# Two-block attention network on one core: input norm's broadcast in two operand parts, final root by Ln and Exp, attention values taken as full pairs of 128 columns

## The chip, the cores and the metric

The kernel runs on one core of a Trainium2 chip. A core has five engines that each work through their own instruction queue: TensorE (matrix products and transposes, its products go to the accumulation memory PSUM), VectorE, ScalarE, GpSimd and SyncE (SP), which here only issues transfers. Transfers between the chip's memory and the on-chip buffers are issued from the queues of SP, ScalarE and GpSimd. The engines wait for each other through semaphores. The metric is the time of one execution on the device, in microseconds (us), and the median over runs is compared. In the views PE is TensorE's products, PEld its loads of the stationary operand, DVE VectorE, ACT ScalarE, POOL GpSimd.

## The reference

The input x has 512 tokens of 1024 features. It is normalized (mean and variance, gain and shift of 1024 elements each) and goes through two layers of a first block and one layer of a second block.

```python
h = _layernorm(x, ln_in_g, ln_in_b)
for layer in range(2):
    proj = h @ w_in[layer]            # aq ak av ag, bq bk bv bf bg, cq ck cv cg
    # a: 4 heads of differential attention, values of 128
    # b: 4 heads of forgetting attention, heads of 64
    #    softmax(q k^T * scale + cum_q - cum_k, causal) @ v
    # c: 4 heads of stick-breaking attention, heads of 64
    #    weights = exp(log_sigmoid(z) + sum of log_sigmoid(-z) over later keys); weights @ v
    y = concat(ya, yb, yc) @ w_out[layer]      # each gated by silu
    h = _layernorm(DEEPNORM_ALPHA * h + y, ln_g[layer], ln_b[layer])
# second block: three mixers (dsa, hgrn2, mla), a gated sum, and a gated feed-forward part
#    mla: s = (q_nope . k_nope + q_pe . k_pe) * scale, q_nope of 128, q_pe of 64; k_pe is one for all 4 heads
x = x + mixed @ w_out_2
x = x + (silu(h @ w_gate) * (h @ w_up)) @ w_down
return rms_norm(x, final_norm)
```

All of it is in float32. `rms_norm` divides by the root of the mean of squares plus 1e-6.

## The kernel before, in words

Tokens are worked in four tiles of 128 (`NT` = 4), and the 1024 features in eight groups of 128 (`KD` = 8). A projection is made in three products of reduced-precision operands: each operand is split into a high part (a cast by ScalarE, line 203 for weights) and a low part (a subtraction by VectorE, line 204), and `mm3` (lines 217 to 219) adds high x high, high x low and low x high. Weights come through SP's queue (line 199) into three buffers `wraw`. Products of attention scores with values, and the transposes ahead of them, are made in full float32.

A scheduler plans a fixed order for each engine from the order of the program and priorities; `self.after(x, y)` only demands that x stands behind y in the order of issue. Generators interleave the side work (an attention mechanism) with main work (projections) at fixed rates (`merge`). `Steps` holds the attention back in stages: the scores of one step, then the transposes of the step before, then the products with the values of the step before that.

**Start.** `start` loads x by tiles through SP, and the gain and shift of the input norm through ScalarE's queue as 16 rows of 128 (line 403). Sixteen float32 products (line 411) broadcast these rows to all partitions, into four PSUM banks: `g` in two halves of 512 features, and `b` in two. `norm` makes each tile's statistics: for tile 0 by VectorE (line 427), for the others by sums on ScalarE (line 423) and squares (line 312). `root` takes an approximate inverse root by Ln and Exp on ScalarE (lines 270 and 272) and one correction on VectorE. Four VectorE passes follow (lines 319 and 320, each once for each half). The tile is then transposed (line 293), split (line 297) and projected to the values of mechanism b. `hgrn_bounds`, for the second block, loads two small vectors through ScalarE's queue (lines 441 and 452) and has some eight tiny instructions; the planner has set them at the beginning.

**b and c.** `att_b` takes its 4 heads in 2 pairs. A pair has one PSUM bank `pv` (the tag has one buffer): head 0 of the pair fills partitions 0 to 63, head 1 partitions 64 to 127, for 512 tokens. For each of the 4 token tiles, and in it for each head, the product with the values is made from 64 columns of v (line 787, made in line 1093). After both heads of a pair, `out_bc` multiplies the whole bank by the gate (line 563), and `finish` splits the result. `att_c` goes head by head, each in four key tiles, and puts its products with 64 columns of v into the pair's bank (lines 848 and 852); `out_bc` follows after the second head (line 565).

**mla.** The scores are two products: 128 rows of q and k (line 1372), and the rope part of 64 rows (line 1373). The rope key `kpe` stands twice in one tile, in partitions 0 to 63 and 64 to 127, since the heads' rope queries stand in pairs.

**End.** In `ffn` each of the 4 column groups of 256 adds up its products for the 4 token tiles. In the last third of each group VectorE adds the residual (line 1450), ScalarE squares and sums (line 920), and VectorE multiplies by the gain (line 1452). After the last group `rms_scale` reduces the four sums (line 909), scales them (line 911) and iterates the inverse root three times (`rsqrt`, lines 241 to 265); then ScalarE scales one half of the tile (line 1456) and VectorE the other (line 1458), and both go out.

Of the kernel before, what the change touches and what calls it, by code (L numbers as in the profile page):

```python
# [21 lines left out]
P = 128  # L22
# [13 lines left out]
class Net:  # L36
    def __init__(self, ctx, tc, a, out):
# [8 lines left out]
        self.bounds = None  # L46
# [220 lines left out]
    def root(self, y, s, n, eps, x):  # L267
# [5 lines left out]
        nc.vector.tensor_scalar(x, s, -0.5 / n, -0.5 * eps, op0=ALU.mult, op1=ALU.add)  # L273
        nc.vector.scalar_tensor_tensor(x, y, x, y, op0=ALU.mult, op1=ALU.mult)
        nc.vector.scalar_tensor_tensor(y, x, 1.5, y, op0=ALU.add, op1=ALU.mult)

# [29 lines left out]
    def layernorm(self, x, g, b, eps, mv, sums=True):  # L306

        nc = self.nc
        if sums:
            nc.vector.tensor_scalar(mv[:, 2:3], mv[:, 0:1], mv[:, 1:2], -1.0 / D, op0=ALU.add, op1=ALU.mult)  # L310
            sq = self.wa([P, D], BF16)
            nc.scalar.activation(sq, x, AF.Square, bias=mv[:, 2:3], accum_out=mv[:, 3:4])
            self.root(mv[:, 5:6], mv[:, 3:4], D, eps, mv[:, 4:5])
        else:
            nc.vector.tensor_scalar_mul(mv[:, 2:3], mv[:, 0:1], -1.0)
            self.root(mv[:, 5:6], mv[:, 1:2], 1, eps, mv[:, 4:5])
        for half in range(2):
            y = x[:, half * S:(half + 1) * S]
            nc.vector.scalar_tensor_tensor(y, y, mv[:, 2:3], g[half], op0=ALU.add, op1=ALU.mult)
            nc.vector.scalar_tensor_tensor(y, y, mv[:, 5:6], b[half], op0=ALU.mult, op1=ALU.add)  # L320
# [48 lines left out]
    def values(self, l, hT, w=None, pool=None):  # L369
# [6 lines left out]
        w = w or self.weights(self.src1(l, "bv", 0, 260), 260, pool=pool)  # L376
# [4 lines left out]
        def step(t):  # L381
# [3 lines left out]
            ps = self.proj_n(w, 260, hT, t)  # L385
# [6 lines left out]
    def start(self, hT):  # L392
# [3 lines left out]
        self.roots()  # L396
# [16 lines left out]

        def norm(t):
# [14 lines left out]
            self.layernorm(xs[t], g, b, 1e-5, st, sums=t > 0)  # L429
# [1405 lines left out]
```

## Time and profile before

| | |
|---|---|
| time, median of 3 runs | 1658.45 us (1657.46 to 1660.41) |
| the profiled execution's own time | 1661.47 us |
| its span in the profile | 1659.7 us |
| TensorE busy | 1618.0 us (97%), 9320 products |
| VectorE busy | 1045.5 us (63%), 2281 instructions |
| ScalarE busy | 734.5 us (44%), 1507 instructions |
| mean granted TensorE clock | 0.994 |

A product's record lasts longer than it holds the engine: records overlap, and their ends are modelled, so a busy engine is not an engine at its peak. The distance between starts tells what a record costs the next one. A float32 product stands as two records. Idle time of an engine that is not the bottleneck costs nothing.

### The profile page before, as it was taken

What the parts mean: (1) busy time and instruction counts of PE and PEld (TensorE: products, weight loads), DVE (VectorE), ACT (ScalarE), POOL (GpSimd) and SP (SyncE); (2) the same over time, 40 slices, a digit from 0 to 9 for tenths busy, and PEclk for the clock granted to TensorE, in tenths of its full rate; (3) what the DMA queues carried; (4) which work ended last, traced back from release to release, by engine and by line L of the source; (5) the groups of instructions that cost most, each with busy time, mean ns of one, the idle gap of its engine ahead of it and who ended that gap; (6) DMA issues with size and microseconds to landing.
All of it is one profiled execution on the core that took longest, in us unless ns stands there. A gap on an engine that the chain in (4) does not pass through costs nothing.

```text
span 1659.7 us, 24221 instructions
## 1 busy us (share of the span) xinstructions
PE 1618.0 (97%) x9320; PEld 1374.3 (83%) x9320; DVE 1045.5 (63%) x2281; ACT 734.5 (44%) x1507; POOL 67.0 (4%) x117
## 2 busy tenths in 40 slices
PE   6999999999999999899999999999999999999997
PEld 6878787987777979788889866788889988888997
DVE  7686878884567797836999996433446434434233
ACT  4455654443465644556545765422333322322222
POOL 1021000100000000000000001100000000000000
PEclk9999999999999999999999999999999999999999
DMA  7443132341121413432012321223443533333221
GB/s 230 143 164 107 33 111 75 103 154 56 51 77 39 128 61 122 138 89 79 24 39 69 90 64 52 83 83 108 147 126 105 162 102 101 102 102 96 96 92 61
DMA packets 141884, 160.33 MB, mean 97 GB/s; under 512 B 14101, under 2 KB 131109, under 8 KB 141257
## 3 DMA queue, kind: packets, MB, share of 16 engines
q1 hardware_dynamic: 135960, 141.34, 27.7%
q0 software_dynamic: 2944, 12.13, 2.1%
q10 hardware_dynamic: 2864, 5.32, 1.0%
q8 instruction: 73, 1.20, 0.3%
q14 instruction: 43, 0.34, 0.1%
HBM read 143.55 MB, written 15.21 MB: 96 GB/s over the span
## 4 chain that ended last, share of the span: by engine, by line
PE 83%; DVE 8%; ACT 2%; DMA 1%; issue 1%; ACTq 0%; DVEq 0%
PE pj L218 19%; PE pj L217 19%; PE pj L219 19%; PE pv L1093 3%; PE tr L732 2%; PE s L217 2%; PE s L218 2%; PE s L219 2%; PE s L718 2%; PE s L1685 2%; PE s L719 1%; PE s L837 1%; DVE wlo L204 1%; DMA wraw<-in_w_in_dram 1%; PE pv L848 1%
## 5 line engine op out<-in xcount | busy, mean ns | idle before, releaser
L218 PE MATMUL pj<-hTl,whi 128*128 128x512 f32 (+1 forms) x1136 | 440.8, 388 | 0.0
L217 PE MATMUL pj<-hTh,whi 128*128 128x512 f32 (+1 forms) x1136 | 440.2, 388 | 0.0
L219 PE MATMUL pj<-hTh,wlo 128*128 128x512 f32 (+1 forms) x1136 | 439.6, 387 | 0.2 <-DVE wlo L204 0.2
L204 DVE TENSOR_TENSOR wlo<-wraw,whi 128x1024 fp32r<-128x1024 f32 (+3 forms) x237 | 269.4, 1143 | 240.7 <-ACT whi L203 235.5
L203 ACT CAST whi<-wraw 128x1024 fp32r<-128x1024 f32 (+3 forms) x237 | 228.9, 979 | 333.3 <-PE pj L218 196.8
L217 PEld LDWEIGHTS pj<-hTh,whi 128*128 128x128 f32 x1136 | 213.6, 188 | 45.3 <-issue 6.6
L218 PEld LDWEIGHTS pj<-hTl,whi 128*128 128x128 f32 x1136 | 213.6, 188 | 43.4 <-issue 4.8
L219 PEld LDWEIGHTS pj<-hTh,wlo 128*128 128x128 f32 x1136 | 213.6, 188 | 42.9 <-issue 3.8
L217 PE MATMUL pj<-whi,hTh 128*128 128x256 f32 (+2 forms) x352 | 101.2, 288 | 3.4 <-ACT whi L208 2.7
L219 PE MATMUL pj<-whi,hTl 128*128 128x256 f32 (+2 forms) x352 | 101.9, 290 | 0.0
L218 PE MATMUL pj<-wlo,hTh 128*128 128x256 f32 (+2 forms) x352 | 101.1, 288 | 0.0
L219 PE MATMUL pj<-whi,t2k 128*128 128x256 f32 x304 | 85.7, 282 | 0.0
L218 PE MATMUL pj<-wlo,t2k 128*128 128x256 f32 x304 | 85.6, 282 | 0.0
L217 PE MATMUL pj<-whi,t2k 128*128 128x256 f32 x304 | 85.4, 281 | 0.0
L219 PE MATMUL s<-whi,t2k 128*128 128x256 f32 x264 | 73.8, 280 | 0.0
L217 PE MATMUL s<-whi,t2k 128*128 128x256 f32 x264 | 73.8, 280 | 0.0
L218 PE MATMUL s<-wlo,t2k 128*128 128x256 f32 x264 | 73.8, 280 | 0.0
L217 PEld LDWEIGHTS pj<-whi,hTh 128*128 128x128 f32 x352 | 68.0, 194 | 5.0 <-ACT whi L208 3.3
L219 PEld LDWEIGHTS pj<-whi,hTl 128*128 128x128 f32 x352 | 68.1, 193 | 0.4
L218 PEld LDWEIGHTS pj<-wlo,hTh 128*128 128x128 f32 x352 | 68.1, 194 | 0.3
L735 ACT COPY wa<-tr 128x128 f32<-128x128 f32 (+3 forms) x96 | 40.6, 423 | 58.7 <-PE tr L732 57.3
L723 DVE CUSTOM_DVE_ANT_0 wa<-s,mask 128x128 f32<-128x128 f32 (+3 forms) x112 | 52.6, 486 | 9.0 <-PE tr L732 5.1
(455 smaller groups left out, 3080.0 us busy)
## 6 DMA issues: line engine op xcount, KB each, us to landing
wraw<-in_w_in_dram SPq DMA_DIRECT2D x112, 512.0 KB, 3.8
wraw<-in_w_ffn_gate_dram SPq DMA_DIRECT2D x22, 512.0 KB, 3.6
wraw<-in_w_ffn_up_dram SPq DMA_DIRECT2D x22, 512.0 KB, 4.5
wraw<-in_w_ffn_down_dram SPq DMA_DIRECT2D x16, 512.0 KB, 3.5
tok<-hres SPq DMA_DIRECT2D x12, 512.0 KB, 7.4
wraw<-in_w_out_dram SPq DMA_DIRECT2D x12, 512.0 KB, 4.1
hres<-tok SPq DMA_DIRECT2D x12, 512.0 KB, 2.8
wraw<-in_w_out_dram SPq DMA_DIRECT2D x8, 384.0 KB, 3.0
```

The costliest lines, as they stand in the source:

```text
L203: nc.scalar.copy(hi[:, ka:kb], raw)
L204: nc.vector.tensor_sub(lo[:, ka:kb], raw, hi[:, ka:kb])
L217: nc.tensor.matmul(out, lhsT=wh(k), rhs=xh(k), start=start and k == 0, stop=False)
L218: nc.tensor.matmul(out, lhsT=wh(k), rhs=xl(k), start=False, stop=False)
L219: nc.tensor.matmul(out, lhsT=wl(k), rhs=xh(k), start=False, stop=stop and k == nk - 1)
L718: nc.tensor.matmul(sc, lhsT=stacked[:, rows], rhs=twice[hh][:, cols], start=True, stop=False)
L719: return nc.tensor.matmul(sc, lhsT=stacked[:, rows], rhs=twice[2 + hh][:, cols], start=False, stop=stop)
L723: self.nc.vector.tensor_tensor_reduce(p[:, :w], sc[:, :w], self.maskw[:, S - w:] if mask is None else mask, scale=1.0, scalar=3e38, op0=AL ...
L732: x = nc.tensor.transpose(pt[:, j, :], src[:, j * P:(j + 1) * P], self.ident)
L735: nc.scalar.copy(dst[:, :n, :], pt[:, :n, :])
L1093: x = self.nc.tensor.matmul(out, lhsT=l, rhs=r, start=k == 0, stop=k == i)
L1685: nc.tensor.matmul(ps[:, l, :], lhsT=yk[:, c + l, :], rhs=E[:, c + l, :], start=True, stop=True)
```

## The change

It has four parts.

The gain and shift of the input norm come as four rows of 256 each; they are split into a high and a low part of reduced precision, and eight pairs of products of 256 columns broadcast them from all 128 partitions (the unused rows are zero). Tile 0's root is made by `rsqrt` on VectorE. The first weights' split is issued after tile 0's norm, and the VectorE steps of the norms are put into the order of the tiles and halves by `hold` and `self.normed`. The two small loads of `hgrn_bounds` go to SP's queue, behind the load of the rope table; the table for Ln and Exp is loaded behind the gain's and shift's requests.

In b and c each product with the values takes 128 columns, those of both heads of a pair, and fills all 128 partitions of the bank; half of it is used. b goes head by head, and not tile by tile with two heads. The bank is taken anew for each head, and `out_bc` multiplies half of the bank by half of the gate after each head.

In mla the rope key stands in two tiles, in each with 64 partitions of zeros, and the products take all 128 rows.

At the end, the sums of the first three column groups are added and scaled once the third is there, Ln (with that sum as its bias) and Exp make the approximate root of the whole on ScalarE, and VectorE makes one correction. Their table is loaded behind the last gate's Tanh.

```diff
@@ layernorm
+    def layernorm(self, x, g, b, eps, mv, sums=True, hold=None):
         if sums:
-            nc.vector.tensor_scalar(mv[:, 2:3], mv[:, 0:1], mv[:, 1:2], -1.0 / D, op0=ALU.add, op1=ALU.mult)
+            self.after(nc.vector.tensor_scalar(mv[:, 2:3], mv[:, 0:1], mv[:, 1:2], -1.0 / D, op0=ALU.add, op1=ALU.mult), hold)
             sq = self.wa([P, D], BF16)
             nc.scalar.activation(sq, x, AF.Square, bias=mv[:, 2:3], accum_out=mv[:, 3:4])
-            self.root(mv[:, 5:6], mv[:, 3:4], D, eps, mv[:, 4:5])
+            self.after(self.root(mv[:, 5:6], mv[:, 3:4], D, eps, mv[:, 4:5]), self.normed)
         else:
+            nc.vector.tensor_scalar(mv[:, 4:5], mv[:, 1:2], 0.5, 0.5 * eps, op0=ALU.mult, op1=ALU.add)
             nc.vector.tensor_scalar_mul(mv[:, 2:3], mv[:, 0:1], -1.0)
-            self.root(mv[:, 5:6], mv[:, 1:2], 1, eps, mv[:, 4:5])
+            self.rsqrt(mv[:, 5:6], mv[:, 4:5], 1)
+        before = self.normed
         for half in range(2):
             y = x[:, half * S:(half + 1) * S]
-            nc.vector.scalar_tensor_tensor(y, y, mv[:, 2:3], g[half], op0=ALU.add, op1=ALU.mult)
-            nc.vector.scalar_tensor_tensor(y, y, mv[:, 5:6], b[half], op0=ALU.mult, op1=ALU.add)
+            i = nc.vector.scalar_tensor_tensor(y, y, mv[:, 2:3], g[half], op0=ALU.add, op1=ALU.mult)
+            self.after(i, before)
+            self.normed = nc.vector.scalar_tensor_tensor(y, y, mv[:, 5:6], b[half], op0=ALU.mult, op1=ALU.add)
@@ start
-        gb = self.tok.tile([16, P], F32, name="gb8", tag="gb8")
+        gb = self.tok.tile([P, 256], F32, name="gb8", tag="gb8")
+        gh, gl = (self.tok.tile([P, 256], F32R, name=n, tag=n) for n in ("gb8h", "gb8l"))
+        one = self.tok.tile([P, 8], F32R, name="one", tag="one")
+        nc.vector.memset(gb, 0.0)
+        self.roots()
         for j, name in enumerate(("ln_in_g", "ln_in_b")):
-            nc.scalar.dma_start(gb[8 * j:8 * j + 8], a[name].rearrange("(k n) -> k n", k=8))
+            self.after(self.table, nc.scalar.dma_start(gb[4 * j:4 * j + 4], a[name].rearrange("(k n) -> k n", k=4)))
+        nc.gpsimd.tensor_copy(one, self.ident[:, :8])
         load(0)
-        first = self.weights(self.src1(0, "bv", 0, 260), 260)
+        first = [self.weights(self.src1(0, "bv", 0, 260), 260, later=True)]
         ...
+        nc.vector.tensor_copy(gh, gb)
+        nc.vector.tensor_sub(gl, gb, gh)
         for j, r in enumerate((g, b)):
-            for k in range(8):
-                nc.tensor.matmul(r[k // 4][:, k % 4 * P:k % 4 * P + P], lhsT=self.ident[:16, 8 * j + k:8 * j + k + 1].broadcast_to([16, P]),
-                                 rhs=gb, start=True, stop=True)
+            for k in range(4):
+                o, pick = r[k // 2][:, k % 2 * 256:k % 2 * 256 + 256], one[:, 4 * j + k:4 * j + k + 1].broadcast_to([P, P])
+                nc.tensor.matmul(o, lhsT=pick, rhs=gh, start=True, stop=False)
+                nc.tensor.matmul(o, lhsT=pick, rhs=gl, start=False, stop=True)
@@ start, norm(t)
-            self.layernorm(xs[t], g, b, 1e-5, st, sums=t > 0)
+            self.layernorm(xs[t], g, b, 1e-5, st, sums=t > 0, hold=self.normed)
+            if not t:
+                first[0] = first[0](None, self.normed)
@@ hgrn_bounds (and the same for gb, line 452)
-        nc.scalar.dma_start(lg, a["hgrn_lb_logits_2"][0].rearrange("(h p) -> p h", p=P))
+        self.after(nc.sync.dma_start(lg, a["hgrn_lb_logits_2"][0].rearrange("(h p) -> p h", p=P)), self.roped)
@@ out_bc
-        def out_bc(k, pv, scale):
-            g = gates[k]
+        def out_bc(k, hh, pv, scale):
+            r = slice(hh * 64, hh * 64 + 64)
+            g = gates[k][r]
             if scale == 1.0:
-                nc.vector.tensor_mul(g, pv, g)
+                nc.vector.tensor_mul(g, pv[r], g)
             else:
-                nc.vector.scalar_tensor_tensor(g, pv, scale, g, op0=ALU.mult, op1=ALU.mult)
-            finish(k, g)
+                nc.vector.scalar_tensor_tensor(g, pv[r], scale, g, op0=ALU.mult, op1=ALU.mult)
+            if hh:
+                finish(k, gates[k])
@@ att_b
         for pr in range(2):
-            pv = self.p("pv")
-            for i in range(NT):
-                ...
-                for hh in range(2):
+            vv = lambda k, c=512 + pr * P: v[k][:, c:c + P]
+            for hh in range(2):
+                h = pr * 2 + hh
+                pv = self.p("pv")
+                for i in range(NT):
                     ...
-                    self.step(steps, scored, p, i, pv[r:r + 64, qi], lambda k, h=h: v[k][:, 512 + h * 64:576 + h * 64],
-                              done=(lambda pr=pr, pv=pv: out(4 + pr, pv, 1.0)) if i == NT - 1 and hh else None)
+                    self.step(steps, scored, p, i, pv[:, qi], vv,
+                              done=(lambda pr=pr, hh=hh, pv=pv: out(4 + pr, hh, pv, 1.0)) if i == NT - 1 else None)
@@ att_c, put
-                    if hh == 0 and k == NT - 1:
+                    if k == NT - 1:
                         pvs[pr] = self.p("pv")
                     pv = pvs[pr]
-                    vv = v[k][:, 768 + h * 64:832 + h * 64]
+                    vv = v[k][:, 768 + pr * P:896 + pr * P]
                     with self.lag():
-                        x = nc.tensor.matmul(pv[r:r + 64, k * P:(k + 1) * P], lhsT=vv, rhs=p[:, :P], start=k == NT - 1, stop=False)
+                        x = nc.tensor.matmul(pv[:, k * P:(k + 1) * P], lhsT=vv, rhs=p[:, :P], start=k == NT - 1, stop=False)
                         ...
-                            nc.tensor.matmul(pv[r:r + 64, (k + 1) * P:], lhsT=vv, rhs=p[:, P:], start=False, stop=k == 0)
-                    if hh and k == 0:
-                        out(6 + pr, pv, 0.5)
+                            nc.tensor.matmul(pv[:, (k + 1) * P:], lhsT=vv, rhs=p[:, P:], start=False, stop=k == 0)
+                    if k == 0:
+                        out(6 + pr, hh, pv, 0.5)
@@ attention2
                 kpe = self.rope2_apply(kpr, 64, tab, self.slot())
-                nc.scalar.copy(kpe[64:128], kpe[0:64])
+                kpe = kpe, self.slot()
+                nc.scalar.copy(kpe[1][64:128], kpe[0][0:64])
+                nc.gpsimd.memset(kpe[0][64:128], 0.0)
+                nc.gpsimd.memset(kpe[1][0:64], 0.0)
@@ mla
-                scored = nc.tensor.matmul(sc[:, :w], lhsT=qp[h // 2][r:r + 64, qi], rhs=kpe[r:r + 64, :w], start=False, stop=True)
+                scored = nc.tensor.matmul(sc[:, :w], lhsT=qp[h // 2][:, qi], rhs=kpe[h % 2][:, :w], start=False, stop=True)
@@ ffn
-                    nc.scalar.activation(g, pg, AF.Tanh, scale=0.5)
+                    gate = nc.scalar.activation(g, pg, AF.Tanh, scale=0.5)
         ...
+        self.roots(gate)
         g = self.bcast("fng", a["final_norm_2"], D)
         ...
                         self.squares(rc, 256, sums[t], c)
+                        s = lambda k: sums[t][:, k:k + 1]
+                        if c == 2:
+                            nc.vector.reduce_sum(s(4), sums[t][:, 0:3], axis=AX.X)
+                            nc.vector.tensor_scalar(s(5), s(4), 1.0 / D, 1e-6, op0=ALU.mult, op1=ALU.add)
+                            nc.vector.tensor_scalar_mul(s(7), s(5), -0.5)
+                        if c == 3:
+                            r = s(6)
+                            self.after(nc.scalar.activation(r, s(3), AF.Ln, scale=1.0 / D, bias=s(5)), self.table)
+                            nc.scalar.activation(r, r, AF.Exp, scale=-0.5)
+                            nc.vector.tensor_scalar(s(4), s(3), -0.5 / D, s(7), op0=ALU.mult, op1=ALU.add)
                         nc.vector.tensor_mul(rc, rc, g[:, cs])
                         if c == 3:
-                            self.rms_scale(sums[t], D, 4)
-                            r = sums[t][:, 6:7]
+                            nc.vector.scalar_tensor_tensor(s(4), r, s(4), r, op0=ALU.mult, op1=ALU.mult)
+                            nc.vector.scalar_tensor_tensor(r, s(4), 1.5, r, op0=ALU.add, op1=ALU.mult)
```

## Rows read from the trace of the kernel before

**Rows 1.** The page: shares of the chain that ended last, by engine.
```profile
PE 83%; DVE 8%; ACT 2%; DMA 1%; issue 1%; ACTq 0%; DVEq 0%
```

**Rows 2.** Busy time by stretch (five asked for); the last row is their sum.
```profile
160.00:210.00 50.00, 50.00 (x251) 36.85 (x250) 39.96 (x75) 32.69 (x65) 1.04 (x6) 1.00 0.13 38
...
sum 228.00, PE 228.00 PEld 163.96 DVE 171.16 ACT 129.93 POOL 15.99; mean PE 45.60 PEld 32.79 DVE 34.23 ACT 25.99 POOL 3.20
```

**Rows 3.** Timeline of TensorE in b: start, duration, line, tiles, form, records merged.
```profile
122.00 0.60 PE L732 MATMUL tr<-ident,wa 128*128 128x128 f32 x4
122.53 0.87 PE L1093 MATMUL pv<-wa,v 128*64 128x128 f32 x6
123.33 0.50 PE L217 MATMUL pj<-hTh,whi 128*128 128x512 f32 x1
123.67 0.40 PE L218 MATMUL pj<-hTl,whi 128*128 128x512 f32 x1
123.91 0.40 PE L219 MATMUL pj<-hTh,wlo 128*128 128x512 f32 x1
```

**Rows 4.** Timeline of TensorE in the second block's dsa, all shapes 128 by 128.
```profile
1041.73 0.38 PE L732 MATMUL tr<-ident,wa 128*128 128x128 f32 x2
1041.87 0.48 PE L218 MATMUL pj<-hTl,whi 128*128 128x512 f32 x1
1042.18 0.40 PE L219 MATMUL pj<-hTh,wlo 128*128 128x512 f32 x1
...
1052.91 1.50 PE L1093 MATMUL pv<-wa,av 128*128 128x128 f32 x12
```

**Rows 5.** Timeline of TensorE in c.
```profile
162.92 0.43 PE L848 MATMUL pv<-cz,v 128*64 128x128 f32 x2
163.19 0.38 PE L852 MATMUL pv<-cz,v 128*64 128x128 f32 x2
163.50 0.50 PE L837 MATMUL s<-ch,ntri 128*128 128x512 f32 x1
```

**Rows 6.** Timeline of TensorE in mla.
```profile
1008.74 1.12 PE L1373 MATMUL s<-t2k,ms 64*128 64x512 f32 x2
1009.80 0.49 PE L1093 MATMUL pv<-wa,t2k 128*128 128x128 f32 x2
```

**Rows 7.** Timeline of TensorE in b, the last two steps of a pair.
```profile
126.98 1.83 PE L1093 MATMUL pv<-wa,v 128*64 128x128 f32 x16
```

**Rows 8.** Line 563: durations (ns, min/median/max), and who waited for it (us, times).
```profile
L563 DVE TENSOR_TENSOR g<-pv,g x4: 687/692/693, 109.7 to 448.9; 128x512 f32<-128x512 f32 x4
...
  PEld pv L1093: 0.4, 1
```

**Rows 9.** Timeline of the start; in brackets the idle time before and its releaser.
```profile
5.36 0.28 ACTq L403 DMA_DIRECT2D gb<-in_ln_in_b_dram  x1
...
9.34 3.75 PE L411 MATMUL s<-gb,ident 16*128 16x128 f32 x16 [9.34 <-DMA gb<-in_ln_in_b_dram]
...
11.80 0.63 ACT L423 ACTIVATE wa<-tok 128x512 bf16<-128x512 f32 x1 [1.10 <-DMA tok<-in_x_dram]
...
33.96 0.74 DVE L320 SCALAR_TENSOR_TENSOR tok<-tok,ln_st,s 128x512 f32<-128x512 f32 x1
```

**Rows 10.** Timeline of the end; a one-column Ln; ScalarE's table loads (busy us, mean ns).
```profile
1650.12 0.28 PE L219 MATMUL pv<-whi,t2k 128*128 128x256 f32 x1
1650.98 0.41 DVE L1450 TENSOR_TENSOR tok<-tok,pv 128x256 f32<-128x256 f32 x1
1652.93 0.15 DVE L909 TENSOR_REDUCE rm_s<-rm_s 128x1 f32<-128x4 f32 x1
1655.17 0.72 ACT L1456 ACTIVATE tok<-tok,rm_s 128x512 f32<-128x512 f32 x1 [1.40 <-DVE rm_s L265]
...
24.10 0.30 ACT L270 ACTIVATE ln_st<-ln_st,eps1e-05_81 128x1 f32<-128x1 f32 x1
...
L279 ACT ACT_TABLE_LOAD x3 | 3.8, 1283 | 1.9 <-issue 1.9
```

More of the change, by code (lines that the diff above doesn't have):

```diff
@@ L45, in __init__ @@
         self.n = 0
-        self.bounds = None
+        self.bounds = self.normed = None
         self.setup()
@@ L272, in root @@
         nc.scalar.activation(y, y, AF.Exp, scale=-0.5)
-        nc.vector.tensor_scalar(x, s, -0.5 / n, -0.5 * eps, op0=ALU.mult, op1=ALU.add)
+        first = nc.vector.tensor_scalar(x, s, -0.5 / n, -0.5 * eps, op0=ALU.mult, op1=ALU.add)
         nc.vector.scalar_tensor_tensor(x, y, x, y, op0=ALU.mult, op1=ALU.mult)
         nc.vector.scalar_tensor_tensor(y, x, 1.5, y, op0=ALU.add, op1=ALU.mult)
+        return first
     def roots(self, before=None):
@@ L375, in values @@
         self.vl = v, lf
-        w = w or self.weights(self.src1(l, "bv", 0, 260), 260, pool=pool)
+        w = w or [self.weights(self.src1(l, "bv", 0, 260), 260, pool=pool)]
         if l:
@@ L384, in step @@
                 wc = later(*self.last_split)
-            ps = self.proj_n(w, 260, hT, t)
+            ps = self.proj_n(w[0], 260, hT, t)
             nc.scalar.copy(v[t][:, 512:768], ps[:, 0:256])
@@ L451, in hgrn_bounds @@
         nc.vector.tensor_scalar(kc[:, 4:8], lb, 0.5, -0.5, op0=ALU.mult, op1=ALU.add)
-        nc.scalar.dma_start(gb, a["hgrn_out_norm_2"][0].rearrange("(p o) -> p o", o=1))
+        self.after(nc.sync.dma_start(gb, a["hgrn_out_norm_2"][0].rearrange("(p o) -> p o", o=1)), self.roped)
         nc.vector.tensor_scalar_mul(gb, gb, 0.25)
@@ L481, in small1 @@
         self.rope_a = self.u("rope", [P, 2, S], 1)
-        nc.sync.dma_start(self.rope_a, a["c_rope_a"])
+        self.roped = nc.sync.dma_start(self.rope_a, a["c_rope_a"])
         self.lam, self.gsub = lam, gsub
@@ L770, in att_b @@
         for pr in range(2):
-            pv = self.p("pv")
-            for i in range(NT):
-                w = (i + 1) * P
-                qi = slice(i * P, w)
-                for hh in range(2):
-                    h, r = pr * 2 + hh, hh * 64
+            vv = lambda k, c=512 + pr * P: v[k][:, c:c + P]
[3 more added lines that the diff above has]
+                for i in range(NT):
+                    w = (i + 1) * P
+                    qi = slice(i * P, w)
                     sc = self.p("s")
@@ L827, in sums @@
         def sums(pr, hh, z, hi, lo):
-            h, r = pr * 2 + hh, hh * 64
             for k in range(NT - 1, -1, -1):
@@ L1369, in mla @@
             for h in range(4):
-                r = (h % 2) * 64
                 sc = self.p("s")
                 nc.tensor.matmul(sc[:, :w], lhsT=qn[h][:, qi], rhs=kn[h][:, :w], start=True, stop=False)
-                scored = nc.tensor.matmul(sc[:, :w], lhsT=qp[h // 2][r:r + 64, qi], rhs=kpe[r:r + 64, :w], start=False, stop=True)
+                scored = nc.tensor.matmul(sc[:, :w], lhsT=qp[h // 2][:, qi], rhs=kpe[h % 2][:, :w], start=False, stop=True)
                 st = self.t("st", [P, 4], 6)
```

2 lines of the change are left out of this document (removed).

## The prediction, made before the result was known

> **What bounds the kernel now.** I read the page first, for its chain of waits: it lies on TensorE for 83% of the span and on VectorE for 8% [rows 1]. So a change pays where TensorE's own time shrinks, or where TensorE stands still. Then I asked for the busy time by stage, in the five stretches where the changed attention code runs (first mechanism b and c in both layers, and the second block's mla). TensorE is busy in all 228.0 of their 228.0 us, with no wait listed; VectorE follows, in the densest of them with 39.96 of 50 us [rows 2]. A stretch that is wholly busy can still hide loss, so I went on to the timeline of TensorE alone and looked at distances between starts, not at durations, which overlap. The reader is to see there how long a run of records keeps the next one from starting. Last I read the beginning and the end of the span, where TensorE does wait.
>
> **Values as 128 columns, and mla's keys padded.** In before, the products with the values use 64 of the array's columns, and mla's rope part 64 of its rows; everything around them uses 128 by 128. A record of 128 moving columns costs 0.11 us where nothing changes shape: twelve take 1.50 us and two 0.38, so ten more take 1.12 [rows 4]. A projection record of 512 columns costs 0.24 (from 123.67 to 123.91) [rows 3]. Around a 64-column run more passes. The four transposes ahead of it hold 0.53 us (122.00 to 122.53) in place of 0.44: 0.09 lost. The six records of the run hold 0.80 in place of 0.66: 0.14 lost. The first projection record behind holds 0.34 in place of 0.24: 0.10 lost [rows 3]. That is 0.33 us for each visit to the other shape. Where the same kinds follow each other without a change of shape nothing is lost: two transposes and a projection record take 0.45 us (1041.73 to 1042.18), which is 2 x 0.11 + 0.23 [rows 4]. The c stage shows the same inside its run, 0.58 in place of 0.44 [rows 5]; mla's run of two 512-column records holds 1.06 in place of 8 x 0.11 = 0.88, so 0.18 there and 0.37 with the two edges as in b [rows 6].
>
> The code gives the number of visits: b has 2 pairs x 4 token tiles x 2 heads x 2 layers = 32, of which two stand together (the run of sixteen [rows 7]), so 31; c has 32; mla has 4 x 4 = 16, of which I count 15. The sum is 63 x 0.33 + 15 x 0.37 = 26.4 us. The changed form issues as many records of as many columns, all at 128 by 128: the 0.11 us above is that form, so the wider products cost nothing more.
>
> What it adds: the pair's product with its gate is done by halves, one after each head, so eight more VectorE instructions (2 pairs x 2 stages x 2 layers), each as long as the whole one, 0.69 us [rows 8]; 5.5 us, hidden while VectorE has room. The one accumulation bank must now be emptied after each head and not after each pair. Queued behind a late emptying is the next head's first product and everything behind it on TensorE. The page of before has eight such hand-overs, and the only wait behind one of the four in b is 0.4 us [rows 8]; a product comes two steps after its scores, so I cost the new ones at nothing, and at 0.4 x 8 = 3 us as the bound. mla's second key tile takes one more slot, a copy that was there before, and two fills by GpSimd, which is busy 16 of the 228 us [rows 2]: nothing.
>
> How much of 26.4 comes back: all of it if the other engines keep up. In the densest stretch 16 visits x 0.33 = 5.3 us go, leaving 44.7 us for 39.96 + 2 x 0.69 = 41.3 us of VectorE, 92% [rows 2]. An engine that full, served in order, will sometimes be late. I take 85%, 22.4 us, between half (13) and all.
>
> **Input norm.** The first broadcast product stands until 9.34 us, for the second gain vector, whose request left only at 5.36, behind ScalarE's wait for another small load [rows 9]. The change moves that load (and one more) to SP's queue behind the rope table, so both requests can leave in the first two microseconds and, at the 3.98 us that this one took, land near 5.5: 3.8 us earlier. On SP the two loads cost two issues, 0.28 us each as here [rows 9], ahead of the weights of the next stage, 0.6 us within the bounds below. The broadcast itself takes 3.75 us for its first sixteen records [rows 9], 7.5 for all thirty-two; the new one has 16 products of twice the columns with single-pass operands, somewhere between half of that and all of it, so another 0 to 3.7. Against that stands token tile 1, whose data land at 11.80 in any case [rows 9], the weights' low parts (now behind tile 0's norm on VectorE), and the strict order of the tiles: a tile's root must follow the one before. Tile 0's own root becomes seven tiny VectorE steps in place of two on ScalarE and two or three on VectorE; at 0.30 us each [rows 10] that is about 1.2 us more on VectorE, beside the broadcast, which ends later. The last tile's norm, which starts its last pass at 33.96 now [rows 9], is what TensorE's dense part waits for. I take 4 us earlier. Bounds: 7.5 earlier, and 3 later, if VectorE meets the moved load's eight tiny instructions before its data are there; behind these all of the norms would queue.
>
> **Final root.** The last product starts at 1650.12, the last scaling at 1655.17; between them VectorE starts the last tile's sum at 1650.98 (late, by the tile before), reduces the sums at 1652.93 and iterates to 1655.17, 2.24 us [rows 10]. The new form has Ln and Exp, at the 0.30 us of the same function in the input norm [rows 10], and two tiny VectorE steps, taken at the same 0.30: 1.2 us, so 1.04 us less. It starts before the product with the gain rather than after it, and the partial sum and its scaling are done a column group earlier; at most the 0.58 us from the last record's end (1650.40) to 1650.98 and, for the gain product, half of the 1.95 us from 1650.98 to 1652.93 come on top, 2.6. I take 2. The table for Ln and Exp is loaded behind the last gate, while ScalarE is mostly idle: nothing; without that cover it costs its 1.28 us once [rows 10].
>
> **Sum.** 22.4 + 4 + 2 = 28.4 us. The profiled execution took 1661.47 us (span 1659.7, 1.8 around it), 3.0 over the median of 1658.45. So 1633.1 for a like one, and 1630.0 as median, 1.7% less.
>
> **A rule against it.** Two heads stand back to back in one run of sixteen 64-column records, eight for each half of the array; they take 1.83 us, 0.11 each, the same as one after the other at full width [rows 7]. The Trainium skill, TensorEngine Tiling (Array Packing), in Key Properties, says that different tiles can load and multiply in parallel, which would make the old form the cheaper one and the new form lose that overlap. No run here shows such a halving; by the rule the sum would shrink to what the fourth rival below gives.
>
> **The rivals.**
> 1. As summed, chance 0.66; its own range 1621 to 1638 (all of 26.4 with 7.5 and 2.6 at one end, half of everything at the other).
> 2. VectorE becomes the bound in b and c, chance 0.18. For it: 92% there. Against: TensorE waits for nothing in 228 us now. If half of the 63 visits' time is lost again, 10.4 us, less is left than summed: 18.0 us saved with the rest whole, 1640.
> 3. The lost time does not belong to the shape but to the kind of operand (full against reduced precision), and so stays, chance 0.06. Then 4 + 2 remain: 1652. Against it stands the clean passage in [rows 4].
> 4. The two halves did overlap, chance 0.04. Price at most half of the products: b has 160 records of 0.11 us, 17.6; c 64 such and 48 of one to three times the width, 17.6; half is 17.6 together. 28.4 - 17.6 = 10.8 saved: 1648. The run of sixteen speaks against it.
> 5. Slower, chance 0.04: the hand-over of the bank. TensorE waits at each of the eight new ones for the last product, a queue on VectorE and 0.69 us of emptying. It decides from 28.4 / 8 = 3.6 us each; at 4.5 us it makes +8 us, 1666. Against it: 0.4 us in before [rows 8].
> 6. No change, chance 0.02: the planner of the order lays the same work out worse elsewhere and eats it, 1658.
>
> **The numbers.** 1630, the likeliest. The range reaches over the second case to the near end of the fourth: 1621 to 1644. A measurement of this kernel tells about 0.2%, 3 us. Faster by more: 0.66 + 0.18 + 0.06 + 0.04 = 0.94; within: 0.02; slower: 0.04.
>
> **What would show it.** The forms 128*64 and 64*128 are gone from TensorE's list, but for small ones; four transposes and six products between projection records take 0.44 + 0.66 and not 0.53 + 0.80; each of the five stretches is 3 to 6 us shorter with TensorE still near fully busy and no wait for VectorE's product with the gate. The first norm's first half ends before 14 us, the last tile's last pass starts near 30. From the last record to the last scaling pass some 3 us rather than 5.05. Wrong I would be if the stretches are shorter on paper but idle on TensorE (second), if the passages are as long at full width (third), or if waits on the bank appear (fifth).

## The result, and the profile after

The changed kernel takes 1641.47 us (median of 4, 1640.1 to 1642.45) against 1658.27 for the kernel before on the same chip: ratio 0.9897, 95% interval 0.9885 to 0.991. That is 16.8 us or 1.0% faster, inside the forecast range of 1621 to 1644, but only 60% of the 28.4 us that the forecast summed. The profiled execution took 1642.45 us, its span is 1640.7.

I read the two traces by starts of the same instruction in both, along the span (us; the last column is after minus before):

| start of | before | after | difference |
|---|---|---|---|
| last group of products for the bias tables | 64.22 | 64.27 | 0.0 |
| b of layer 0 done: third gate, VectorE | 131.07 | 130.10 | -1.0 |
| c of layer 0 done: a copy to v, ScalarE | 237.53 | 232.67 | -4.9 |
| layer 1 begins: lf, VectorE | 383.94 | 380.00 | -3.9 |
| b of layer 1 done: a gate, ScalarE | 452.94 | 445.92 | -7.0 |
| c of layer 1 done: a copy to v, ScalarE | 560.26 | 549.34 | -10.9 |
| second block begins: hTl, VectorE | 689.42 | 677.61 | -11.8 |
| ahead of mla: weight load for pj from lr | 945.90 | 934.16 | -11.7 |
| mla runs: a product pj from lr | 970.54 | 957.23 | -13.3 |
| mla done: oc, ScalarE | 1015.95 | 997.76 | -18.2 |
| last product | 1650.12 | 1632.70 | -17.4 |
| end of span | 1659.7 | 1640.7 | -19.0 |

So in this pair of executions the start gave nothing, b 1.0 and 3.1, c 3.9 twice, mla 4.9, the end 1.6. Some 2 us are given back between these places (at the end of layer 0, and behind mla). And 2.8 us of the 19.0 lie in code that the change leaves alone, where this execution of before met a lower clock, as the last section shows; that is about the gap between the 16.8 of the medians and the 19.0 of the spans.

**The shape.** The forms 128\*64 and 64\*128 are gone from b, c and mla. The timeline of TensorE after, in b; it answers to [rows 3]:

```profile
92.74 0.60 PE L749 MATMUL tr<-ident,wa 128*128 128x128 f32 x4
93.17 0.83 PE L1111 MATMUL pv<-wa,v 128*128 128x128 f32 x6
93.76 0.48 PE L219 MATMUL pj<-hTh,wlo 128*128 128x512 f32 x1
94.08 0.40 PE L217 MATMUL pj<-hTh,whi 128*128 128x512 f32 x1
```

From the first transpose to the second projection record it is 1.34 us; before it was 1.67 (122.00 to 123.67). The difference is 0.33, as summed for one visit: 0.43 + 0.59 + 0.32 in place of 0.53 + 0.80 + 0.34. The parts are not those of the sum, though: 0.10 + 0.21 + 0.02 in place of 0.09 + 0.14 + 0.10. The first projection record behind the products takes 0.32 us at full width too, and the six products lose more than was worked out; that the total agrees is luck. Next c, which answers to [rows 5], and mla, which answers to [rows 6]:

```profile
161.31 0.40 PE L219 MATMUL pj<-hTh,wlo 128*128 128x512 f32 x1
161.55 0.38 PE L866 MATMUL pv<-cz,v 128*128 128x128 f32 x2
161.77 0.39 PE L870 MATMUL pv<-cz,v 128*128 128x128 f32 x2
161.94 0.50 PE L855 MATMUL s<-ch,ntri 128*128 128x512 f32 x1
...
991.20 1.02 PE L1394 MATMUL s<-t2k,ms 128*128 128x512 f32 x2
992.06 0.39 PE L1111 MATMUL pv<-wa,t2k 128*128 128x128 f32 x2
992.28 0.38 PE L749 MATMUL tr<-ident,wa 128*128 128x128 f32 x2
```

In c the four products now hold 0.39 in place of 0.58, in mla the rope part 0.86 in place of 1.06.

**The stretches.** The windows of before and then of after, each from the same work to the same work (b of layer 0, c of layer 0, b of layer 1); behind the length stand the busy times of PE, PEld, DVE, ACT and POOL with their counts, the granted clock, the transfers' share and GB/s:

```profile
87.00:130.00 43.00, 42.97 (x240) 33.21 (x241) 34.07 (x99) 22.54 (x55) 11.63 (x18) 1.00 0.53 183
150.00:237.50 87.50, 86.99 (x504) 70.64 (x503) 70.92 (x155) 56.27 (x122) 5.08 (x12) 1.00 0.23 73
399.00:452.00 53.00, 52.87 (x283) 40.05 (x282) 31.47 (x84) 26.86 (x63) 2.87 (x4) 1.00 0.21 60
```

```profile
87.00:129.00 42.00, 39.83 (x237) 32.44 (x237) 35.50 (x100) 22.43 (x53) 11.63 (x18) 1.00 0.53 177
149.06:232.60 83.54, 82.95 (x504) 72.14 (x503) 71.85 (x157) 56.22 (x122) 5.09 (x12) 1.00 0.25 76
395.00:445.00 50.00, 49.20 (x284) 40.74 (x282) 32.44 (x85) 27.05 (x63) 2.87 (x4) 1.00 0.23 64
```

The same 504 records of TensorE in c's stretch take 4.0 us less and leave TensorE as busy as before (0.6 and 0.5 us idle). In b TensorE is idle for 2.2 us in layer 0 (42.00 less 39.83) where it was hardly ever idle (0.03), and for 0.8 in layer 1 (0.1 before). Its waits in b of layer 0, after (in all, times, longest):

```profile
PE pv L1111 <- DVE g L579: 0.9, 1, 0.9
PE tr L749 <- ACT g L564: 0.8, 1, 0.8
PE s L735 <- DVE t2k L728: 0.4, 1, 0.4
```

The first is the hand-over of the bank: the next head's product waits for the half gate product. The second is ScalarE, with a gate's Tanh queued ahead of what a transpose needs. Before, the same stretch listed only the third of these, 0.4 us too.

**The start.** It answers to [rows 9]. TensorE, ScalarE and VectorE after, with the idle time before and its releaser in brackets, and the windows behind (columns as above):

```profile
11.13 0.74 DVE L325 SCALAR_TENSOR_TENSOR tok<-tok,ln_st,pv 128x512 f32<-128x512 f32 x1
...
13.71 0.58 PE L217 MATMUL pj<-whi,hTh 128*128 128x260 f32 x1 [0.68 <-ACT hTh L298]
...
22.16 1.04 ACT L203 CAST whi<-wraw 128x1024 fp32r<-128x1024 f32 x1 [1.70 <-DMA wraw<-in_w_in_dram]
22.63 0.23 DVE L483 CUSTOM_DVE_ANT_0 lam_u<-lam_u,lam_v 128x64 f32<-128x64 f32 x1 [2.10 <-DMA lam_v<-in_lambda_k_dram]
23.11 0.58 ACT L298 CAST hTh<-tr 128x512 fp32r<-128x512 f32 x1
23.74 0.58 PE L217 MATMUL pj<-whi,hTh 128*128 128x260 f32 x1 [2.46 <-ACT hTh L298]
...
35.26 0.74 DVE L325 SCALAR_TENSOR_TENSOR tok<-tok,ln_st,s 128x512 f32<-128x512 f32 x1
```

```profile
20.00:25.00 5.00, 2.42 (x15) 1.92 (x15) 2.64 (x8) 3.30 (x8) 0.53 (x1) 0.83 0.52 162
25.00:30.00 5.00, 5.00 (x25) 5.00 (x24) 4.97 (x15) 2.17 (x9) 1.02 (x3) 0.50 0.73 221
```

The first projection starts at 13.71, 5.1 us before its place in the old trace (18.78). But ScalarE stands at the cast of the *next* weights until they land, VectorE stands at a small vector's product until its load lands, and the split of token tile 1 is queued behind both. TensorE is idle for 2.46 us, and behind that its clock is granted at 0.50, the lower of its two levels (1.2 GHz of 2.4), for five microseconds and more; before, it was at 1.00 there. The last pass of the norms starts at 35.26, 1.3 us *later* than before.

How much is lost differs from execution to execution. In a second trace of the changed kernel (the run "once more" below) and in one with the new start alone, the last pass starts at 33.57 and 33.22, 0.4 and 0.7 us earlier than before, and the last group for the bias tables at 62.49 and 62.19, 1.7 and 2.0 earlier:

```profile
62.49 1.44 PE L1055 MATMUL s<-bh,bt 128*128 128x512 f32 x5
...
62.19 1.44 PE L1052 MATMUL s<-bh,bt 128*128 128x512 f32 x5
```

A part of it is given back at the end of layer 0. There ScalarE's cast of the next weights waits longer for its load, VectorE's norm of the last tile stands behind their low part, and TensorE's transposes wait for that norm. The cast before, and the cast and the transposes after:

```profile
366.20 1.05 ACT L203 CAST whi<-wraw 128x1024 fp32r<-128x1024 f32 x1 [0.18 <-DMA wraw<-in_w_in_dram]
...
362.26 1.05 ACT L203 CAST whi<-wraw 128x1024 fp32r<-128x1024 f32 x1 [1.11 <-DMA wraw<-in_w_in_dram]
...
367.74 0.66 PE L294 MATMUL s<-ident,tok 128*128 128x128 f32 x4 [0.71 <-DVE tok L325]
```

The new start alone shows the same (1.05 and 0.7 us); b and c alone do not (0.40, and no wait of the transposes). So this loss comes with the new start. Why the load lands later there is not shown.

**The end** answers to [rows 10]:

```profile
1632.70 0.28 PE L219 MATMUL pv<-whi,t2k 128*128 128x256 f32 x1
1633.02 0.42 DVE L1472 TENSOR_TENSOR tok<-tok,pv 128x256 f32<-128x256 f32 x1 [0.56 <-PE pv L219]
1635.70 0.72 ACT L1489 ACTIVATE tok<-tok,rm_s 128x512 f32<-128x512 f32 x1 [0.19 <-issue]
```

From the last product to the last scaling it is 3.0 us in place of 5.05. Of these 2.05 us the span keeps 1.6 (1640.7 less 1632.70, against 1659.7 less 1650.12): the last transfers out, now of two tiles at once, end 0.5 us later behind the scaling.

### The profile page after: what moved, and what is told of

It is laid out like the page before. It is cut to its first block, busy times and chain, and to the rows that moved or that the text cites. A ratio compares the mean times of both kernels' runs of the same rounds, so it can differ in the third digit from the quotient of the medians.

```text
span 1640.7 us, 24217 instructions
## 1 busy us (share of the span) xinstructions
PE 1597.0 (97%) x9304; PEld 1376.3 (84%) x9304; DVE 1048.7 (64%) x2285; ACT 738.1 (45%) x1514; POOL 68.6 (4%) x120
## 5 line engine op out<-in xcount | busy, mean ns | idle before, releaser
L204 DVE TENSOR_TENSOR wlo<-wraw,whi 128x1024 fp32r<-128x1024 f32 (+1 forms) x235 | 266.6, 1141 | 244.2 <-ACT whi L203 241.4
L203 ACT CAST whi<-wraw 128x1024 fp32r<-128x1024 f32 (+1 forms) x235 | 227.0, 979 | 327.5 <-PE pj L218 183.4
L218 PEld LDWEIGHTS pj<-wlo,t2k 128*128 128x128 f32 x304 | 57.2, 188 | 0.3
```

The costliest lines, as they stand in the source:

```text
L203: nc.scalar.copy(hi[:, ka:kb], raw)
L204: nc.vector.tensor_sub(lo[:, ka:kb], raw, hi[:, ka:kb])
L218: nc.tensor.matmul(out, lhsT=wh(k), rhs=xl(k), start=False, stop=False)
```

## The experiments

Each ratio is against the kernel before on the same chip, with its 95% interval; the microseconds are the ratio's share of that kernel's median there (1659 to 1661).

**The four parts one by one.** Each is the kernel before with the lines of one part of the change, as they stand in the diff above.

```diff
 e1_mla
-                scored = nc.tensor.matmul(sc[:, :w], lhsT=qp[h // 2][r:r + 64, qi], rhs=kpe[r:r + 64, :w], start=False, stop=True)
+                scored = nc.tensor.matmul(sc[:, :w], lhsT=qp[h // 2][:, qi], rhs=kpe[h % 2][:, :w], start=False, stop=True)
 e2_vals
-            finish(k, g)
+            if hh:
+                finish(k, gates[k])
 e3_start
-            self.layernorm(xs[t], g, b, 1e-5, st, sums=t > 0)
+            self.layernorm(xs[t], g, b, 1e-5, st, sums=t > 0, hold=self.normed)
 e4_tail
-                            self.rms_scale(sums[t], D, 4)
+                            nc.vector.scalar_tensor_tensor(s(4), r, s(4), r, op0=ALU.mult, op1=ALU.mult)
+                            nc.vector.scalar_tensor_tensor(r, s(4), 1.5, r, op0=ALU.add, op1=ALU.mult)
```

> The kernel before with the padded rope key of mla alone. If the lost time belongs to the change of shape, 15 visits of 0.37 us come back: 5.6 us, 1652.7; the comparison of the two traces puts 5.9 us on this stretch. If it belongs to the kind of operand, nothing changes: 1658. If VectorE or the two fills eat it, between 0 and 3 us.

> The kernel before with the 128-column values of b and c alone (head order, hand-over of the bank after each head and the halved gate product with them). The forecast's term was 17.8 us (63 visits of 0.33 us, 85%): 1640.5. The two traces put some 4 us on b and 8 on c: 12 us, 1646. If b's loss in the whole change came from the start (other work shifted into b), this one gives the 17.8 us; if it belongs to the head order, 12 us here too.

> The kernel before with the new input norm, and the two small loads on SP's queue, alone. The forecast's term was 4 us: 1654. The trace of after shows a lead of 5 us at the first projection that is gone by 62 us: then 1658, within 1.5 us. If the waits of VectorE and ScalarE for loads cost more than the lead, up to 3 us slower: 1661.

> The kernel before with the new final root alone. The forecast's term was 2 us, the two traces show 1.6 at the end: 1656.5. If the table load behind the last gate is not hidden, 1.3 us less: 1657.9.

Measured: mla 0.9969 (0.9957 to 0.9981), 5.1 us less; b and c 0.9925 (0.9911 to 0.9938), 12.5 us less; start 0.9995 (0.9985 to 1.0005), 0.8 us less and not told from nothing; end 0.9982 (0.9973 to 0.9992), 3.0 us less. The lost time belongs to the shape and not to the kind of operand, for mla changes the shape alone; the start is worth next to nothing alone too; b and c give 12.5 us without the other parts (10.3 to 14.8 by the interval), so most of their lack against 17.8 does not come from the start. The end alone (1.3 to 4.5 us by its interval) agrees with the 1.6 of the traces. The four add up to 21.4 us against 17.1 for the whole (the changed kernel once more, below); each is uncertain by some 2 us, so a loss between the parts is possible and not shown.

**b and c one by one.** The same for the products of `att_b` or of `att_c` alone; the other keeps 64 columns and hands over after the pair.

```diff
 e11_b
-                    self.step(steps, scored, p, i, pv[r:r + 64, qi], lambda k, h=h: v[k][:, 512 + h * 64:576 + h * 64],
+                    self.step(steps, scored, p, i, pv[:, qi], vv,
 e12_c
-                    vv = v[k][:, 768 + h * 64:832 + h * 64]
+                    vv = v[k][:, 768 + pr * P:896 + pr * P]
```

> The kernel before with the 128-column values in b alone (head order, hand-over and halved gate product with them). The forecast's term for b was 31 visits of 0.33 us, 85%: 8.7 us, 1649.5. By the distances in the traces the shape's loss goes and 1.6 to 2.9 us of waits for VectorE and ScalarE come in its place in each layer: 4 to 5 us less than the kernel before, 0.3%.

> The kernel before with the 128-column values in c alone (bank and halved gate product after each head). The forecast's term for c was 32 visits of 0.33 us, 85%: 9.0 us. By the distances in the traces a visit in c costs 0.25 us, 8.0 together, and the waits hardly grow: 8 us less than the kernel before, 0.5%; if the halved gate product or the hand-over bites here too, 5 to 6 us.

Measured: b 0.9961 (0.9949 to 0.9973), 6.5 us less; c 0.9954 (0.9942 to 0.9966), 7.6 us less. c is as expected. b lies between the 8.7 of the forecast, which is just outside its interval (4.5 to 8.5 us), and the 4 to 5 read from the traces, of which the upper end is just inside it.

**The order of b apart from its shape**, in both directions: the new order at 64 columns on the kernel before, and the old order at 128 columns on the changed kernel, with zeros in the other head's place so that one bank serves the pair again. (To make room for the zeros, `pick` is held as one column a head.)

```diff
 e7_order
-                for hh in range(2):
+            for hh in range(2):
+                pv = self.p("pv")
+                for i in range(NT):
 e6_pad
+        vb = [x[:, 512:896].rearrange("p (a b c) -> p a b c", a=2, b=3) for x in v]
+        for x in vb:
+            nc.gpsimd.memset(x[:, :, 1], 0.0)
-            for hh in range(2):
-                pv = self.p("pv")
-                for i in range(NT):
+            pv = self.p("pv")
+            for i in range(NT):
+                for hh in range(2):
-                    self.step(steps, scored, p, i, pv[:, qi], vv,
+                    self.step(steps, scored, p, i, pv[:, qi], lambda k, c=512 + pr * 192 + hh * 64: v[k][:, c:c + P], group=(not hh, hh),
```

> The changed kernel once more, as the measure for the two that are built on it: 1.0% below the kernel before, 1641.5.

> The kernel before, with b alone in the new order: head by head, the bank taken for each head, the gate product in two halves, and still 64 columns. If this order costs what b's gain lacks, 3 to 5 us slower than the kernel before: 1662. If the order is free and the lack is elsewhere, no change: 1658.

> The changed kernel, with b alone in the old order (token tile by token tile, the two heads in turn) and still 128 columns: the values of a pair stand as v0, zeros, v1, so that each head's 128 columns carry zeros in the other's place, and both heads add into one bank, which is handed over once a pair with one gate product. If the head-by-head order with its hand-over and halved gate products ate b's gain, b saves its whole 4.5 to 5 us in each layer and not 1 and 3: 5 to 6 us less, 1636. If VectorE's load or the planner ate it, 0 to 1.5 us less: 1640 to 1641.5.

Measured: the changed kernel once more 0.9897 (0.9883 to 0.9912); the order alone 0.9999 (0.9989 to 1.0008); the old order with padded values 0.9883 (0.9866 to 0.9899), 2.5 us under the changed kernel by the medians, the intervals overlapping. "If the order is free" seems to be the answer, but the trace of the order alone tells more. Its products stand together more often, in 23 runs of 64 columns over both layers in place of 31, the longest in the middle of this row of b in layer 0:

```profile
110.82 2.40 PE L1095 MATMUL pv<-wa,v 128*64 128x128 f32 x20 [0.78 <-DVE g L564]
```

Eight visits fewer at 0.33 us are 2.6 us gained by the price of a visit, and the time is the same, so the order seems to cost about as much in waits: TensorE is idle for 1.2 us of 87 to 130 and 0.8 of 398.5 to 451.5, where it was idle for 0.03 and 0.1 before, 0.8 of it at this hand-over.

Not all of the 2.5 us that the old order gives back at 128 columns lies in b. In that trace the last group for the bias tables, ahead of b, starts at 61.22, earlier than in both traces of the changed kernel (64.27 and 62.49), so a part is the start's, which differs between executions. The distances over the stretches with b (us; in layer 0 from that group to c's copy to v, in layer 1 from lf to the gate, as in the first table) leave it out:

| | layer 0, b and c | layer 1, b |
|---|---|---|
| before | 173.31 | 69.00 |
| the order alone, 64 columns | 173.10 | 68.09 |
| b alone | 171.19 | 65.92 |
| b and c alone | 167.54 | 65.93 |
| the changed kernel, two traces | 168.40, 168.24 | 65.92, 65.95 |
| it with the old order, padded | 167.13 | 65.44 |

So the old order gives back 1.1 to 1.3 us in layer 0 and 0.5 in layer 1. My theory holds for some 1.6 to 1.8 of the 4.6 us that b lacks, and not for the 5 to 6 that I had put on it. Another 0.7 to 0.9 us in layer 0 is there when b and c stand on the old start, and not on the new one. With the old order back TensorE still waits in b of layer 0, at other places (1.6 us listed, after 2.1):

```profile
PE tr L752 <- DVE wa L1099: 0.7, 1, 0.7
PE s L738 <- DVE t2k L731: 0.5, 1, 0.5
PE s L738 <- DVE st L743: 0.4, 1, 0.4
```

All three are waits for VectorE, two of them for steps of the softmax. So a TensorE that is quicker in b seems to run into the softmax chain by either order, and the new order adds the hand-over to it; no run separates the two.

**The start.** First I took away the loads that VectorE stood at: `hgrn_bounds`' two loads go to GpSimd's queue, the small vectors get eight buffers, and VectorE's work on them is issued behind the last norm. Then also the casts of the next weights, behind the split of token tile 1, and the last small pieces of work on loaded data behind the last norm.

```diff
 e5_fix
-        self.after(nc.sync.dma_start(lg, a["hgrn_lb_logits_2"][0].rearrange("(h p) -> p h", p=P)), self.roped)
-        nc.vector.tensor_sub(e, lg, lg)
+        nc.gpsimd.dma_start(lg, a["hgrn_lb_logits_2"][0].rearrange("(h p) -> p h", p=P))
+        self.after(nc.vector.tensor_sub(e, lg, lg), self.normed)
-                u = pool.tile([P, 64], F32, name=self.nm("lam_u"), tag="lam", bufs=2)
+                u = pool.tile([P, 64], F32, name=self.nm("lam_u"), tag="lam", bufs=8)
 e9_hold, beyond e5_fix
+            ws = held and [(self.weights(src(*p), p[2], later=True)(*held), p[2]) for p in parts]
+            self.after(nc.vector.tensor_scalar_mul(gsub[:, l:l + 1], gsub[:, l:l + 1], 0.5 * (1.0 - li)), self.normed)
```

> The changed kernel, with what stands in the way of its start taken out: the two small loads leave from GpSimd's queue instead of ahead of the next weights on SP, the small vectors have eight buffers instead of two, and VectorE's instructions that wait for these loads stand behind the last tile's norm. If the lead of 5 us at the first projection was lost to in-order waits for these loads (2.10 us on VectorE, 1.70 and 0.91 us on ScalarE) and to the half clock behind TensorE's idle 2.46 us, 3 to 5 us come back: 1637 to 1638.5. If the last tile's norm is bound by the work of the tiles itself, or the bias tables bound the stretch up to 60 us, nothing: 1641.5.

> The changed kernel with the run before last but two (small loads elsewhere, their VectorE work behind the last norm) and, beyond it, ScalarE's casts of the next weights, and VectorE's subtractions for them, issued behind the split of token tile 1, so that no engine meets a load ahead of the norms' work; also the scaling of the small gain vector and the first work on the positions stand behind the last norm. If the casts that wait for the weights (2.86 and 0.34 us in that run, 1.70 and 0.91 in the changed kernel) are what stops TensorE in the start, its idle 3.6 us goes, and the half clock behind it: 3 to 5 us under the changed kernel, 1637 to 1639. If the start is bound by the norms' own chain, nothing: 1641.5 to 1642.5.

> Both together: that start, and b in the old order with padded values. If the two add up, 2.5 us from b and 3 to 5 from the start under the changed kernel: 1634 to 1636. If the start gives nothing, 1639.4 as b's part alone.

Measured: the first step alone 0.9902 (0.9886 to 0.9918), no gain over the changed kernel's 0.9897 on the same chip. VectorE no longer stands at the products of the small vectors (it waits for a small gain vector instead, 1.43 us at 17.44), but their eight requests now go out ahead of the next weights, whose own request moves from 12.79 to 14.59 us; ScalarE waits for them longer, and TensorE with it:

```profile
14.59 1.32 SPq L199 DMA_DIRECT2D wraw<-in_w_in_dram  x2
...
21.47 1.05 ACT L203 CAST whi<-wraw 128x1024 fp32r<-128x1024 f32 x1 [2.86 <-DMA wraw<-in_w_in_dram]
...
25.57 0.59 PE L217 MATMUL pj<-whi,hTh 128*128 128x260 f32 x1 [3.58 <-ACT hTh L298]
```

The second step on top gives 0.9878 (0.9861 to 0.9894), some 3 us under the changed kernel by the ratios; the intervals overlap a little, and the two were measured on different chips. The windows of this run, where the changed kernel had 2.42 and 5.00 us of busy TensorE at a clock of 0.83 and 0.50:

```profile
20.00:25.00 5.00, 4.29 (x31) 3.66 (x30) 3.00 (x8) 3.52 (x10) 0.53 (x1) 1.00 0.90 277
25.00:30.00 5.00, 3.54 (x26) 3.13 (x27) 4.82 (x12) 4.97 (x11) 2.01 (x5) 1.00 0.64 209
```

TensorE issues 57 records there in place of 40, at the full clock. The last group of products for the bias tables, in the kernel before, after, with this start, and with this start and the padded values:

```profile
64.22 1.43 PE L1037 MATMUL s<-bh,bt 128*128 128x512 f32 x5
```

```profile
64.27 1.44 PE L1055 MATMUL s<-bh,bt 128*128 128x512 f32 x5
```

```profile
60.52 1.44 PE L1062 MATMUL s<-bh,bt 128*128 128x512 f32 x5
```

```profile
59.90 1.43 PE L1064 MATMUL s<-bh,bt 128*128 128x512 f32 x5
```

Against the kernel before the 4 us of the forecast are there at this place, 3.7 by these rows, once no engine meets a load ahead of the norms. Against the changed kernel it is 3.7 or 2.0, by which of its two traces is taken, and at the end of layer 0 the wait of the transposes stays (1.1 us). Both together take 1637.42 us, ratio 0.9861 (0.9845 to 0.9878), 23 us under the kernel before and the fastest of all that ran; 6 us under the changed kernel by the ratios, as expected, with intervals that do not touch.

## Why the forecast held, and where its sum was off

**The mechanism was right**: a visit to the other shape costs TensorE time, and the change takes all visits away. The third rival (kind of operand) falls with mla alone. The fourth (halves that overlap) falls with b alone: it would have lost such an overlap and been slower by up to 9 us, and it is 6.5 us faster. c can't tell, since its heads stand one after the other in either form. The Trainium skill, TensorEngine Tiling (Array Packing), Key Properties, says that changing the tiling mode drains TensorE; these 0.33 us agree. The overlap of tiles that the same list states did not show here: sixteen records in the two halves took 0.11 us each [rows 7].

The range held because it was drawn up to 1644 for the second rival. The likeliest case's own range ended at 1638, short of the measured 1641.47; "half of everything", by which its end was named, would be 13.2 + 2 + 1 = 16.2 us or 1642. And the fifth rival's sign, a wait on the bank, did appear, at one hand-over of b and at 0.9 us, far from the 3.6 each that would have decided it. Of the five stretches that were to be 3 to 6 us shorter, b of layer 0 is not (1.0).

**Sizes**, against the profiled execution, 19.0 us saved where 28.4 were summed:
- mla: 0.37 x 15 x 85% = 4.7 summed, 4.9 in the traces, 5.1 alone. Right, with two errors that cancel: a visit is worth 4.9 / 15 = 0.33 and not 0.37, and nothing of it was lost again.
- c: 0.33 x 32 x 85% = 9.0 summed, 7.8 in the traces, 7.6 alone. The visit's price was carried over from b; in c it is 4.0 / 16 = 0.25. VectorE was as full as worked out (92%), and did not stop TensorE there; after, 46.40 of 50.00 us beside 49.63 of TensorE:

```profile
160.00:210.00 50.00, 49.63 (x276) 41.80 (x276) 46.40 (x93) 36.15 (x73) 2.44 (x8) 1.00 0.15 43
```

- b: 0.33 x 31 x 85% = 8.7 summed, 4.1 in the traces, 6.5 alone. The step that failed is the 85% here, with "hidden while VectorE has room" and the hand-over "at nothing". That is the second rival in part, in b and not in c, where I had put it, and by waits for VectorE and ScalarE without a full VectorE: it is busy 35.50 of 42.00. Of the 4.6 us lacking, the new order makes 1.6 to 1.8 and the new start 0.7 to 0.9, by the distances above; the rest, some 2 us, stays open, with waits for the softmax chain as the likeliest cause.
- end: 2 summed, 1.6 in the trace. "Some 3 us rather than 5.05" came out as 3.0.
- start: 4 summed; 0.0 in this trace, 1.7 in the second trace and 2.0 alone at the bias tables, of which some 1 is lost again at the end of layer 0; 0.8 alone over the whole run, not told from nothing. The first half of it was right, tile 0's norm ends its first half at 11.87, before the 14 that I named. The step that failed is "the last tile's norm ... I take 4 us earlier": it came 1.3 later in this trace, and 0.4 and 0.7 earlier in the two others. The bound "3 later, if VectorE meets the moved load's eight tiny instructions" named the kind of trap and the wrong load: the moved load had landed, and a small vector's and above all the next weights' had not. With TensorE early, the planned order put their work ahead of the norms' while the data came no sooner, so most of the 5.1 us gained at the front became waits, all of them in this trace. The Trainium skill, PSUM — Partial Sum Buffer, Engine vs sequencer instructions, says that the queues of ScalarE, VectorE and GpSimd are strictly first in, first out; the trace agrees, with hTh at 23.11 directly behind the cast that waited 1.70 us.

Of the 2 us given back, 1.0 at the end of layer 0 comes with the new start, as shown above. The 0.8 behind mla is chance: from mla's end to the last scaling the second trace of the changed kernel is 0.8 us shorter than the first.

## What to carry to other kernels

The distance between starts shows a loss that busy time hides, and it could be forecast here to within a tenth of a microsecond for each visit (0.33 in b and mla, 0.25 in c, where 0.33 to 0.37 was summed); price it at each place, since the neighbours differ. Before crediting a stage with time that another engine gets back, look at the latency of the chain that feeds it, not only at how full the feeding engine is. And when the front of a kernel moves earlier, list every instruction there that waits for a load: whatever stands behind it on its engine waits too, so either its load or its place has to move as well.

## What the hardware showed beside

The same wait need not have the same effect on the clock. In code that the change doesn't touch, ahead of mla, TensorE waits 1.85 us for ScalarE in both kernels; behind it the granted clock is 0.63 in this execution of before and 1.00 in that of after, which makes 1.6 us. Before, then after:

```profile
964.47 0.49 PE L1372 MATMUL s<-ms,t2k 128*128 128x128 f32 x2 [1.85 <-ACT ms L1576]
...
964.00:968.00 4.00, 3.53 (x12) 3.04 (x13) 4.00 (x8) 3.68 (x6) 0.00 (x0) 0.63 0.21 66
```

```profile
952.74 0.49 PE L1393 MATMUL s<-ms,t2k 128*128 128x128 f32 x2 [1.85 <-ACT ms L1609]
...
952.26:956.26 4.00, 3.52 (x18) 3.04 (x19) 3.99 (x9) 3.94 (x7) 0.00 (x0) 1.00 0.23 66
```

The wait is 1.85 or 1.86 us in all fourteen traces of this document. Behind it the granted clock over four microseconds is 0.58 to 0.68 in four of them (before, mla alone, and the two with the padded values) and 1.00 in the other ten.

A later rise of the clock just ahead of the second block makes another 1.2 us between the same two executions (one instruction starts at 676.83 and 666.24, the next in the table at 689.42 and 677.61). So one profile against another can be wrong by 3 us here without any change in the code, as much as the whole part at the end is worth.
